# A decoder layer on one core: splitting 544 tokens 256 and 288, with the high and low halves of the first part in one 512-column product

## The chip, the cores and the metric

The kernel runs on one core of a Trainium2 chip. The metric is the device time of one launch in microseconds (us), as the median of several runs. One of the runs is taken with the hardware profiler; its page and its trace are what this document reads. The granted TensorE clock of a stretch is shown as a share of the full 2.4 GHz: 1.00 is 2.4 GHz, 0.50 is 1.2 GHz.

## What is computed

One layer of a hybrid decoder on 544 tokens (one prompt of 512 and eight samples of 4), with width 1024 and feed-forward width 2816:

```
x <- LN(alpha*x + gate0 * 0.5*SwiGLU1(mod0(x)))
x <- LN(alpha*x + gate1 * W_out[ GDN_heads(u) || ShortConv_groups(u) ])   u = mod1(x), one combined W_in
x <- LN(alpha*x + gate2 * 0.5*SwiGLU2(mod2(x)))
with mod_i(h) = h*(1+scale_i(c)) + shift_i(c),  swiglu(u) = (silu(u @ wg) * (u @ wu)) @ wd
```

Inputs and outputs are float32, the states of the recurrences among them.

## The kernel before

Activations lie with the features on the 128 partitions and the 544 tokens along the free axis; 1024 features are 8 blocks (`KC`). To get float32 accuracy from the one-pass float32r products, each weight tile is split into a high part (`whi`, cast by ScalarE, L195) and a rest (`wlo`, a VectorE subtraction, L196), and so is each activation (`uh`, `ul`; `bh`, `bl`; `hxh`, `hxl`; by `split`, L258 and L259). `mm3` (L199 to L211) then makes three products for each pair of a weight tile and a feature block: high by high, high by low, low by high, all added in one PSUM tile. The 544 tokens pass in two parts of 272 columns (`HB`), so a pair costs six products. Every product is recorded at L75, the wrapper `PE.matmul`.

```
ins = PE.matmul(o, lhsT=hi[:, i, :], rhs=xh[:, c], start=first and i == 0, stop=False)
PE.matmul(o, lhsT=hi[:, i, :], rhs=xl[:, c], start=False, stop=False)
PE.matmul(o, lhsT=lo[:, i, :], rhs=xh[:, c], start=False, stop=last and i == n - 1)
```

`ffn` (L453) runs twice. It treats the 22 blocks of the hidden width in two halves of 11. For each block, `up` makes the gate tile `pg` and the up tile `pu` for the first part of the tokens and then for the second (8 feature blocks each); ScalarE takes the Silu of `pg` (L474), VectorE multiplies it by `pu` (L476), and the product is split for the down products. For each of 8 output blocks the down products add up 11 hidden blocks, and `residual` (L414) adds the PSUM tile, times the gate, to the residual `z` on VectorE (L419; the 32 sample tokens apart, L422 and L425). So a feed-forward block has 22 x 2 x 8 up pairs and 16 x 11 down pairs, 528 in all, and the two have 1056.

The last three output blocks of a feed-forward block (the last four of the mixer) pass through `finish_stage` (L428), where the layer norm's sums are formed while the last products run: `ln_shift` (L307) for both parts, then per block `ln_sums` (L333), then `ln_stats` (L338), whose two product groups `aux<-s` and `aux<-v` stand between the products of the second part on TensorE and wait for VectorE's sums (L335, L304).

The `mixer` (L520) makes the projections with `proj` (L544), convolutions on VectorE, the gated delta rule, and for the eight samples a chain of rounds that load a state (`s0u`), update it and write it out; each round has its products `vm,kd` on TensorE. One of the short-convolution tiles (`wide`, L553, asked for at L1047 for j == 3) is made with 512 + 32 columns for its first four feature blocks and 364 + 148 + 32 for the other four, instead of 272 + 272. `out_proj` (L1120) then reads the saved residual back from DRAM (`ax_d`) and rescales it on GpSimd (L410).

PSUM has four `acc` tiles, two that swing between uses, and two `aux` tiles. A scheduler (Tile) fixes each engine's order at build time; engines run their own lists in order and wait on one another by semaphores.

Of the kernel before, what the change touches and what calls it, by code (L numbers as in the profile page):

```python
# [23 lines left out]
HB = T // 2  # L24
HP = TP - HB
# [38 lines left out]
def trunk_step(ctx: ExitStack, tc: tile.TileContext, xin, cin, par_d, cst_d, msk_d, wada, wg1, wu1,  # L64
# [134 lines left out]
    def mm3(pt, w, x, ks, hf, first=True, last=True, pin=None):  # L199
        hi, lo = w  # L200
        c = slice(hf * HB, (hf + 1) * HB)
        n = len(ks)
        for i, k in enumerate(ks):
            o = pt[:, 0:HB]
            xh, xl = x(k)
            ins = PE.matmul(o, lhsT=hi[:, i, :], rhs=xh[:, c], start=first and i == 0, stop=False)
            if pin and k in pin:
                after(ins, pin[k], "the next group's modulation first")
            PE.matmul(o, lhsT=hi[:, i, :], rhs=xl[:, c], start=False, stop=False)
            PE.matmul(o, lhsT=lo[:, i, :], rhs=xh[:, c], start=False,  # L210
                      stop=last and i == n - 1)  # L211
# [13 lines left out]
    uh = acts.tile([P, KC, T], F32R, name="uh")  # L225
    ul = acts.tile([P, KC, T], F32R, name="ul")
    bh = acts.tile([P, KC, T], F32R, name="bh")
    bl = acts.tile([P, KC, T], F32R, name="bl")
    ax_d = dram.tile([P, KC, T], F32, name="ax_d")
    rs_d = dram.tile([P, 2, HB], F32, name="rs_d")  # L230
# [14 lines left out]
    def uin(k):  # L245
        return uh[:, k, :], ul[:, k, :]

    def heads(k):
        return bh[:, k, :], bl[:, k, :]
# [48 lines left out]
    def acc_squares(v2, x, n, first):  # L298
        if first:
            A.activation(v2[:, 0:n], x, AF.Square)  # L300
            return
        sqk = st["pool"].tile([P, 2, HB], F32, tag="sqk", name="sqk")
        A.activation(sqk[:, 0:n], x, AF.Square)
        V.tensor_tensor(v2[:, 0:n], v2[:, 0:n], sqk[:, 0:n], ALU.add)  # L304


    def ln_shift(hf, nd):  # L307
        z, lnp = st["z"], st["pool"]
        c = slice(hf * HB, (hf + 1) * HB)
        s1 = lnp.tile([P, HB], F32, tag="s1", name="s1")  # L310
# [4 lines left out]
        sr = lnp.tile([P, HB], F32R, tag="ms", name="s1r", bufs=1)  # L315
        A.copy(sr, s1)
        pm = aux()
        PE.matmul(pm[:, 0:HB], lhsT=st["oned"], rhs=sr, start=True, stop=True)
        m1 = lnp.tile([P, HB], F32, tag="rs", name="m1")
        A.mul(m1, pm[:, 0:HB], float(KC) / nd)  # L320
        v2 = lnp.tile([P, 2, HB], F32, tag="v2", name="v2")
        for k in range(0, nd, 2):
            n = min(2, nd - k)
            zz = z[:, k:k + n, c]
            V.tensor_tensor(zz, zz, m1.unsqueeze(1).to_broadcast([P, n, HB]), ALU.subtract)  # L325
            acc_squares(v2, zz, n, k == 0)
# [6 lines left out]
    def ln_sums(k, hf, sv):  # L333
        c = slice(hf * HB, (hf + 1) * HB)
# [3 lines left out]
    def ln_stats(i, hf, sv):  # L338
        z, lnp = st["z"], st["pool"]
        c = slice(hf * HB, (hf + 1) * HB)  # L340
        s1, v2 = sv
        pm, pv = aux(), aux()
        PE.matmul(pm[:, 0:HB], lhsT=cst["oned"], rhs=s1, start=True, stop=True)
        PE.matmul(pv[:, 0:HB], lhsT=cst["oned"], rhs=v2[:, 0], start=True, stop=True)
        rs = lnp.tile([P, HB], F32, tag="rs", name="rs")
        a, nt = v2[:, 0], v2[:, 1]
        A.activation(nt, pm[:, 0:HB], AF.Square)
        ms = lnp.tile([P, HB], F32, tag="ms", name="ms", bufs=1)
        A.copy(ms, pm[:, 0:HB])
        V.scalar_tensor_tensor(a, pv[:, 0:HB], LN_EPS, nt, ALU.add, ALU.subtract)  # L350
# [3 lines left out]
        for k in range(0, 4, 2):  # L354
            zz = z[:, k:k + 2, c]
            V.tensor_tensor(zz, zz, pm[:, 0:HB].unsqueeze(1).to_broadcast([P, 2, HB]), ALU.subtract)
# [7 lines left out]
    def ln_apply(i, hf, q, pr_):  # L364
        z, lnp = st["z"], st["pool"]
        c = slice(hf * HB, (hf + 1) * HB)
        if i == 2:
            for k0 in range(0, KC, 2):
                ks = (k0, k0 + 1)
                zz = z[:, k0:k0 + 2, c]  # L370
                rr = pr_.unsqueeze(1).to_broadcast([P, 2, HB])
# [10 lines left out]
        np_ = HB if hf == 0 else HP  # L382
        pc = slice(hf * HB, hf * HB + np_)
        for k in range(KC):
            u = lnp.tile([P, HB], F32, tag="lnu", name="lnu", bufs=3)
# [10 lines left out]
            if hf and k == 0:  # L396
# [3 lines left out]
                                pr_[:, HP:HB].unsqueeze(1).to_broadcast([P, KC, TS]), ALU.mult)  # L400
# [5 lines left out]
    def ln_residual(i, hf, q, rb):  # L406
        z = st["z"]
        c = slice(hf * HB, (hf + 1) * HB)
# [5 lines left out]
    def residual(d, hf, pd, i):  # L414
        z = st["z"]
        gt = mod[:, i * 3 + 2, d, :]
        np_ = HB if hf == 0 else HP
        pc = slice(hf * HB, hf * HB + np_)
        V.scalar_tensor_tensor(z[:, d, pc], pd[:, 0:np_], gt[:, 0:1], z[:, d, pc], ALU.mult, ALU.add)  # L419
        if hf:  # L420
            t4 = tmp.tile([P, 8, 4], F32, tag="zs", name="zs")
            V.tensor_tensor(t4, pd[:, HP:HB].rearrange("p (b t) -> p b t", t=4), bc4(gt[:, 1:9]),  # L422
# [5 lines left out]
    def finish_stage(i, nd, half_of, q, fill):  # L428
# [14 lines left out]
        if i == 0:  # L443

            nc.sync.dma_start(out=rs_d[:, 0, :], in_=ra)
            nc.sync.dma_start(out=rs_d[:, 1, :], in_=rb)
            for hf in range(2):
                c = slice(hf * HB, (hf + 1) * HB)
# [4 lines left out]
    def ffn(i, wg, wu, wd, extra, pre, fill):  # L453
        pool = st["pool"]
        xh = pool.tile([P, NFH - KC, T], F32R, tag="hxh", name="hxh", bufs=1)
        xl = pool.tile([P, NFH - KC, T], F32R, tag="hxl", name="hxl", bufs=1)

        def hid(k):
            return (bh[:, k, :], bl[:, k, :]) if k < KC else (xh[:, k - KC, :], xl[:, k - KC, :])

        def up(fs, half, extra_units):
# [5 lines left out]
            for hf in range(2):  # L467
                c = slice(hf * HB, (hf + 1) * HB)
                for f, (w1, w2) in zip(fs, us):
                    pg, pu = acc(), acc()  # L470
                    mm3(pg, w1, uin, range(KC), hf, pin=pin)
                    mm3(pu, w2, uin, range(KC), hf, pin=pin)
                    sg = pool.tile([P, HB], F32, tag="sg", name="sg")
                    A.activation(sg, pg[:, 0:HB], AF.Silu)  # L474
# [815 lines left out]
```

## Time and profile before

| | |
|---|---|
| runs | 1247.17, 1249.36 and 1244.53 us, median 1247.17 |
| profiled execution | 1243.21 us, of which the span from first to last instruction is 1241.5 us |
| granted TensorE clock, mean | 0.983 |
| TensorE (PE) busy | 1181.2 us, 95% of the span |
| VectorE (DVE) busy | 637.9 us, 51% |
| ScalarE (ACT) busy | 451.8 us, 36% |
| chain that ended last | PE 77%, DVE 10%, DMA 4% |

The page gives each engine's busy time, the chain of work that ended last, and groups of instructions with their count and mean duration. A product's recorded duration (about 290 ns) contains its passage through the array and overlaps its neighbours'; what a product costs in a dense stream is the distance from one start to the next, which is read from counts in a window, or from two starts. PEld is the loading of weights, which runs beside the products.

### The profile page before, as it was taken

Reading aid. Unit: us, or ns where it says so; the run is one execution under the profiler, and the core shown is the slowest. Engines: PE = TensorE matmul, PEld = TensorE weight load, DVE = VectorE, ACT = ScalarE, POOL = GpSimd, SP = SyncE. Lnnn points to the kernel's source line nnn. Section 1 sums busy time; section 2 is a strip of 40 time slices with the busy share of each in tenths; the row PEclk is TensorE's granted clock in tenths of the full one; section 3 lists DMA queues with packets and bytes.
Section 4 is the critical chain, followed back from the end, with each engine's and each line's share of the span. In section 5 each row is a group of like instructions: output and inputs, shape, how many; then the busy total and the mean of one; then the engine's idle time right before and its main releaser. Section 6 shows DMA issues by size and latency. Waiting matters only on the chain.

```text
span 1241.5 us, 22584 instructions
## 1 busy us (share of the span) xinstructions
PE 1181.2 (95%) x9238; PEld 1123.7 (91%) x9238; DVE 637.9 (51%) x1449; ACT 451.8 (36%) x975; POOL 119.4 (10%) x168
## 2 busy tenths in 40 slices
PE   5999999999999989999999999869999999999994
PEld 2888889998999988989999888769999999999994
DVE  4533333333333488758787674993333343333467
ACT  3432222223332245744663324563322222322243
POOL 0000000000000034111120003560000000000024
PEclk9999999999999989999999999889999999999997
DMA  9876554355322224331332454123322333322222
GB/s 348 281 279 226 201 183 150 97 170 204 87 80 71 82 89 156 95 105 47 88 88 72 120 158 156 37 70 101 97 70 71 95 105 94 95 77 77 71 58 72
DMA packets 69383, 149.66 MB, mean 121 GB/s; under 512 B 12576, under 2 KB 33312, under 8 KB 69280
## 3 DMA queue, kind: packets, MB, share of 16 engines
q1 hardware_dynamic: 69280, 148.23, 37.8%
q8 instruction: 72, 1.18, 0.4%
q14 instruction: 31, 0.25, 0.1%
HBM read 139.07 MB, written 9.14 MB: 119 GB/s over the span
## 4 chain that ended last, share of the span: by engine, by line
PE 77%; DVE 10%; DMA 4%; issue 3%; POOL 2%; ACT 2%; SPq 1%; DVEq 0%; POOLq 0%; ACTq 0%
PE acc L75 49%; PE accs L75 19%; PE aux L75 6%; PE auxs L75 2%; DMA xt<-xt_d 1%; DVE wlo L196 1%; PE aux L80 1%; POOL z L410 1%; DMA out_ss<-s0u 1%; DVE ct L679 1%; DVE pb L757 1%; DVE z L325 1%; DVE lnu L386 1%; DMA z<-in_x 1%; POOL z L353 1%
## 5 line engine op out<-in xcount | busy, mean ns | idle before, releaser
L75 PE MATMUL acc<-uh,wlo 128*128 128x272 f32 (+1 forms) x1404 | 406.5, 291 | 7.8 <-DVE wlo L196 7.8
L75 PE MATMUL acc<-uh,whi 128*128 128x272 f32 (+1 forms) x1404 | 411.5, 295 | 1.2 <-ACT uh L258 1.2
L75 PE MATMUL acc<-ul,whi 128*128 128x272 f32 (+1 forms) x1404 | 405.8, 291 | 1.0 <-POOL ul L391 0.4
L195 ACT CAST whi<-raw 128x512 fp32r<-128x512 f32 (+2 forms) x366 | 198.3, 574 | 338.4 <-PE acc L75 203.7
L196 DVE TENSOR_TENSOR wlo<-raw,whi 128x512 fp32r<-128x512 f32 (+2 forms) x366 | 229.4, 645 | 170.6 <-ACT whi L195 162.5
L75 PEld LDWEIGHTS acc<-uh,whi 128*128 128x128 f32 x1404 | 264.8, 189 | 16.1 <-DVE wlo L196 7.5
L75 PEld LDWEIGHTS acc<-uh,wlo 128*128 128x128 f32 x1404 | 264.4, 189 | 10.6 <-DVE wlo L196 9.5
L75 PEld LDWEIGHTS acc<-ul,whi 128*128 128x128 f32 x1404 | 265.1, 189 | 2.6 <-POOL ul L391 0.9
L75 PE MATMUL accs<-uh,wlo 128*128 128x272 f32 x440 | 127.4, 290 | 3.7 <-DVE wlo L196 3.7
L75 PE MATMUL accs<-ul,whi 128*128 128x272 f32 x440 | 127.3, 289 | 0.6 <-DVE ul L259 0.6
L75 PE MATMUL accs<-uh,whi 128*128 128x272 f32 x440 | 127.5, 290 | 0.0
L75 PE MATMUL acc<-bl,whi 128*128 128x272 f32 x416 | 120.4, 290 | 1.2 <-DVE bl L259 1.2
L75 PE MATMUL acc<-bh,whi 128*128 128x272 f32 x416 | 120.9, 291 | 0.0
L75 PE MATMUL acc<-bh,wlo 128*128 128x272 f32 x416 | 120.2, 289 | 0.0
L476 DVE TENSOR_TENSOR h<-acc,sg 128x272 f32<-128x272 f32 x62 | 27.4, 442 | 148.5 <-PE acc L75 147.5
L328 POOL TENSOR_TENSOR z<-z,m 128x272 f32<-128x272 f32 x20 | 22.6, 1162 | 774.1 <-ACT m L320 773.3
L75 PEld LDWEIGHTS accs<-uh,wlo 128*128 128x128 f32 x440 | 83.3, 189 | 4.2 <-DVE wlo L196 4.2
L75 PEld LDWEIGHTS accs<-uh,whi 128*128 128x128 f32 x440 | 83.4, 190 | 1.9 <-ACT oned_r L277 0.8
L75 PEld LDWEIGHTS accs<-ul,whi 128*128 128x128 f32 x440 | 83.3, 189 | 0.8 <-DVE ul L259 0.8
L75 PEld LDWEIGHTS acc<-bl,whi 128*128 128x128 f32 x416 | 78.9, 190 | 1.6 <-DVE bl L259 1.4
L75 PEld LDWEIGHTS acc<-bh,whi 128*128 128x128 f32 x416 | 78.8, 190 | 1.3 <-DVE hxl L259 0.8
L75 PEld LDWEIGHTS acc<-bh,wlo 128*128 128x128 f32 x416 | 78.7, 189 | 0.0
(395 smaller groups left out, 1752.6 us busy)
## 6 DMA issues: line engine op xcount, KB each, us to landing
raw_ada<-in_wada SPq DMA_DIRECT2D x72, 512.0 KB, 6.5
raw<-in_wg SPq DMA_DIRECT2D x44, 512.0 KB, 4.1
raw<-in_wu SPq DMA_DIRECT2D x44, 512.0 KB, 3.7
raw<-in_win SPq DMA_DIRECT2D x29, 512.0 KB, 3.8
raw<-in_wd SPq DMA_DIRECT2D x32, 384.0 KB, 3.2
raw<-in_wd SPq DMA_DIRECT2D x32, 320.0 KB, 2.9
raw<-in_wout SPq DMA_DIRECT2D x8, 512.0 KB, 3.8
z<-in_x SPq DMA_DIRECT2D x8, 272.0 KB, 7.6
```

The costliest lines, as they stand in the source:

```text
L75: return nc.tensor.matmul(out, lhsT=lhsT, rhs=rhs, **kw)
L80: return nc.tensor.transpose(out, x, ident)
L195: A.copy(hi[:, a:b], raw[:, a:b])
L196: V.tensor_tensor(lo[:, a:b], raw[:, a:b], hi[:, a:b].bitcast(F32), ALU.subtract)
L325: V.tensor_tensor(zz, zz, m1.unsqueeze(1).to_broadcast([P, n, HB]), ALU.subtract)
L328: G.tensor_tensor(z[:, k, c], z[:, k, c], m1, ALU.subtract)
L353: G.tensor_tensor(z[:, k, c], z[:, k, c], ms, ALU.subtract)
L386: V.scalar_tensor_tensor(u[:, 0:np_], z[:, k, pc], q["G"][:, k, 0:1], pr_[:, 0:np_], ALU.mult, ALU.mult)
L410: G.tensor_tensor(z[:, k, c], z[:, k, c], rb, ALU.mult)
L476: V.tensor_tensor(h, pu[:, 0:HB], sg, ALU.mult)
L679: V.scalar_tensor_tensor(ct, cb[:, s:s + 568], w[:, s:s + 1], ct, ALU.mult, ALU.add)
L757: V.tensor_tensor(t[:, b], a[:, b].unsqueeze(2).to_broadcast([32, s, s, s]), x[:, b].rearrange("p k c -> p c k").unsqueeze(1).to_broadcast ...
```

## The change

The split of the tokens becomes 256 and 288 (`HP`, `HW`, `CUT`). The high and low halves of an activation become one tile with two planes (`ux`, `bx`, `hx`). In the two feed-forward blocks (`side=True`) the first part of a pair takes two products instead of three: the high weights times both planes as one moving operand of two runs of 256 columns, which fills a PSUM tile of 512; and the low weights times the high plane, added to the upper half of that tile. The two halves of the tile are added later: in `up` by two ScalarE copies and two VectorE additions, in `residual` by a second pass of its VectorE instruction. The second part, the mixer and the output projection keep three products for each pair and part, of 288 and 256 columns. The short-convolution tile in pieces goes.

```
 def mm3(pt, w, x, ks, hf, first=True, last=True, pin=None, side=False):
...
+            if side and hf == 0:
+                ops = [(hi, xx[:, :, c], pt.rearrange("p (s t) -> p s t", s=2)),
+                       (lo, xx[:, 0, c], pt[:, HP:2 * HP])]
+            else:
+                ops = [(hi, xx[:, 0, c], o), (hi, xx[:, 1, c], o), (lo, xx[:, 0, c], o)]
+            for m, (wt, rhs, out) in enumerate(ops):
+                ins = PE.matmul(out, lhsT=wt[:, i, :], rhs=rhs, start=begin and m == 0,
+                                stop=end and m == len(ops) - 1)
...
 def residual(d, hf, pd, i, side=False):
...
-        V.scalar_tensor_tensor(z[:, d, pc], pd[:, 0:np_], gt[:, 0:1], z[:, d, pc], ALU.mult, ALU.add)
+        for n in range(2 if side and hf == 0 else 1):
+            V.scalar_tensor_tensor(z[:, d, pc], pd[:, n * HP:n * HP + np_], gt[:, 0:1], z[:, d, pc],
+                                   ALU.mult, ALU.add)
...
 def up(fs, half, extra_units):
...
-                    A.activation(sg, pg[:, 0:HB], AF.Silu)
-                    h = pool.tile([P, HB], F32, tag="h32", name="h32", bufs=3)
-                    V.tensor_tensor(h, pu[:, 0:HB], sg, ALU.mult)
+                    h = pool.tile([P, HW[hf]], F32, tag="h32", name="h32")
+                    if hf == 0:
+                        A.copy(sg, pg[:, HP:2 * HP])
+                        A.copy(h, pu[:, HP:2 * HP])
+                        V.tensor_tensor(sg, pg[:, 0:HP], sg, ALU.add)
+                        A.activation(sg, sg, AF.Silu)
+                        V.tensor_tensor(h, pu[:, 0:HP], h, ALU.add)
+                        V.tensor_tensor(h, h, sg, ALU.mult)
+                    else:
+                        A.activation(sg, pg[:, 0:HW[hf]], AF.Silu)
+                        V.tensor_tensor(h, pu[:, 0:HW[hf]], sg, ALU.mult)
...
-            pb = yield from proj(16 + j, wide=j == 3)
+            pb = yield from proj(16 + j)
```

On TensorE, in the up products of a feed-forward block, the stream of one tile passes from the first part of the tokens to the second like this. First before (each pair a triple of 272 columns; the names are the PSUM tile, then activation and weight), then in the change:

```order
L75 MATMUL acc<-uh,whi 128x272
L75 MATMUL acc<-ul,whi 128x272
L75 MATMUL acc<-uh,wlo 128x272
L75 MATMUL acc<-uh,whi 128x272
L75 MATMUL acc<-ul,whi 128x272
```

```order
L77 MATMUL acc<-ux,whi 128x512
L77 MATMUL acc<-ux,wlo 128x256
L77 MATMUL acc<-ux,whi 128x512
L77 MATMUL acc<-ux,wlo 128x256
L77 MATMUL acc<-ux,whi 128x288 x2
L77 MATMUL acc<-ux,wlo 128x288
L77 MATMUL acc<-ux,whi 128x288 x2
```

A pair has now two products in the first part and three in the second, where there were three and three.

On ScalarE, in the second feed-forward block, the order around one hidden block in the change (L485 and L486 are the copies from the gate and the up tile, L488 the Silu of the sum, L266 the split of the product, L197 the casting of weights, L492 the Silu of the second part):

```order
L485 COPY sg<-acc 128x256
L488 ACTIVATE sg<-sg 128x256
L486 COPY h_9441<-acc 128x256
L266 CAST bx<-h_9441 128x256
L197 CAST whi<-raw 128x512
L492 ACTIVATE sg<-accs 128x288
```

The Silu of the first part now waits for a VectorE addition, and the weight cast stands behind it.

On TensorE at the end of the second feed-forward block, before and in the change, the sums' products `aux<-s` and `aux<-v` stand among the down products of the second part (`bh`, `bl`, `bx`, `hx` are the hidden blocks):

```order
L75 MATMUL accs<-bl,whi 128x272
L75 MATMUL accs<-bh,wlo 128x272
L75 MATMUL aux<-s_13306,cst_oned 128x272
L75 MATMUL aux<-v_13317,cst_oned 128x272
L75 MATMUL accs<-bh,whi 128x272
```

```order
L77 MATMUL accs<-bx,whi 128x288 x2
L77 MATMUL accs<-bx,wlo 128x288
L77 MATMUL accs<-hx,whi 128x288
L77 MATMUL aux<-s_12464,cst_oned 128x256
L77 MATMUL aux<-v_12475,cst_oned 128x256
L77 MATMUL accs<-hx,whi 128x288
```

Before, they stand behind 12 products of the second part; now they stand behind 25. On VectorE the second passes of `residual` (three in this stage, L428) stand ahead of the last sums that they wait for.

## Rows read from the trace of the kernel before

**Rows 1.** The page: busy time; then the chain that ended last, by engine.

```profile
PE 1181.2 (95%) x9238; PEld 1123.7 (91%) x9238; DVE 637.9 (51%) x1449; ACT 451.8 (36%) x975; POOL 119.4 (10%) x168
...
PE 77%; DVE 10%; DMA 4%; issue 3%; POOL 2%; ACT 2%; SPq 1%; DVEq 0%; POOLq 0%; ACTq 0%
```

**Rows 2.** Windows: stretch, length, busy us (instructions) per engine, clock, DMA share, GB/s.

```profile
200.00:300.00 100.00, 100.00 (x800) 95.24 (x799) 37.26 (x89) 26.17 (x55) 0.00 (x0) 1.00 0.43 136
1100.00:1200.00 100.00, 100.00 (x801) 100.00 (x800) 40.42 (x93) 29.34 (x66) 0.00 (x0) 1.00 0.26 75
```

**Rows 3.** The chain that ended last, pieces in order of time: start, us, what.

```profile
838.54 6.02 PE acc L75 x48
```

**Rows 4.** Timeline of TensorE around the tile in pieces: start, us, engine, what.

```profile
734.88 0.29 PE L75 MATMUL acc<-uh,wlo 128*128 128x272 f32 x1
735.01 0.41 PE L75 MATMUL acc<-uh,whi 128*128 128x512 f32 x2
...
736.66 0.51 PE L75 MATMUL acc<-uh,whi 128*128 128x512 f32 x2
737.02 0.49 PE L75 MATMUL acc<-ul,whi 128*128 128x512 f32 x2
...
738.05 0.50 PE L75 MATMUL acc<-ul,whi 128*128 128x512 f32 x2
...
742.06 0.54 PE L75 MATMUL acc<-ul,whi 128*128 128x364 f32 x3
742.45 0.54 PE L75 MATMUL acc<-uh,wlo 128*128 128x364 f32 x3
```

**Rows 5.** Timeline of the weight loads of the same tile.

```profile
735.24 0.30 PEld L75 LDWEIGHTS acc<-ul,whi 128*128 128x128 f32 x2
...
737.34 0.19 PEld L75 LDWEIGHTS acc<-uh,wlo 128*128 128x128 f32 x1
...
737.45 0.19 PEld L75 LDWEIGHTS acc<-uh,wlo 128*128 128x128 f32 x1
737.68 0.30 PEld L75 LDWEIGHTS acc<-uh,whi 128*128 128x128 f32 x2
```

**Rows 6.** Groups by shape, VectorE and ScalarE, 900 to 1000 us: busy, mean ns | idle before.

```profile
L476 DVE TENSOR_TENSOR h<-acc,sg 128x272 f32<-128x272 f32 x6 | 2.7, 442 | 15.6 <-PE acc L75 15.6
...
L419 DVE SCALAR_TENSOR_TENSOR z<-acc,mod,z 128x272 f32<-128x272 f32 x3 | 1.5, 501 | 7.8 <-PE acc L75 7.8
...
L474 ACT ACTIVATE sg<-acc 128x272 f32<-128x272 f32 x6 | 2.4, 396 | 3.5 <-PE acc L75 3.5
```

**Rows 7.** The chain that ended last, at the mixer's end.

```profile
743.81 3.67 DMA s0u<-in_ssm
...
749.46 3.92 DMA out_ss<-s0u
754.39 3.15 DMA z<-ax_d
757.62 11.60 POOL z L410 x15
```

**Rows 8.** Timeline of TensorE at the sums of both blocks; the bracket is its wait.

```profile
457.42 1.27 PE L75 MATMUL aux<-s,cst_oned 128*128 128x272 f32 x2 [3.32 <-DVE s L335]
...
1213.45 0.98 PE L75 MATMUL aux<-s,cst_oned 128*128 128x272 f32 x2 [3.36 <-DVE s L335]
```

**Rows 9.** The chain that ended last, after the last down product.

```profile
1227.26 0.47 DVE z L419
...
1229.94 0.44 DVE v L350
...
1233.79 2.00 DVE z L372 x3
```

**Rows 10.** Windows: the opening of the second feed-forward block, and cold stretches (columns as in rows 2).

```profile
800.00:850.00 50.00, 38.58 (x259) 35.89 (x259) 42.97 (x75) 30.63 (x67) 24.59 (x26) 0.90 0.25 74
...
828.10:831.50 3.40, 3.08 (x12) 2.76 (x12) 3.40 (x7) 1.69 (x6) 2.29 (x3) 0.50 0.53 154
1213.80:1217.20 3.40, 3.40 (x14) 3.05 (x13) 1.74 (x4) 1.10 (x3) 1.98 (x3) 0.50 0.00 0
```

**Rows 11.** What TensorE waited for, 795 to 840 us: total, times, longest.

```profile
PE acc L75 <- DVE wlo L196: 7.0, 5, 3.7
PE accs L75 <- DVE wlo L196: 2.0, 1, 2.0
```

More of the change, by code (lines that the diff above doesn't have):

```diff
@@ L23 @@
 T = TP + TS
-HB = T // 2
-HP = TP - HB
+HP = 256
+HW = (HP, T - HP)
+CUT = (slice(0, HP), slice(HP, T))
 NF = 22
@@ L197, in unit, with mm3 @@
         return hi, lo
-    def mm3(pt, w, x, ks, hf, first=True, last=True, pin=None):
+    def mm3(pt, w, x, ks, hf, first=True, last=True, pin=None, side=False):
         hi, lo = w
-        c = slice(hf * HB, (hf + 1) * HB)
+        c = CUT[hf]
         n = len(ks)
+        o = pt[:, 0:HW[hf]]
         for i, k in enumerate(ks):
[L204 to L211, printed above, removed]
+            xx = x(k)
+            begin, end = first and i == 0, last and i == n - 1
+            if side and hf == 0:
[6 more added lines that the diff above has]
+                                stop=end and m == len(ops) - 1)
+                if pin and k in pin and m == 0:
+                    after(ins, pin[k], "the next group's modulation first")
     def rsqrt(out, x, shape, eps, scale=1.0):
@@ L381, in ln_apply @@
             return
-        np_ = HB if hf == 0 else HP
-        pc = slice(hf * HB, hf * HB + np_)
+        np_ = HP
+        pc = slice(hf * HP, hf * HP + np_)
         for k in range(KC):
-            u = lnp.tile([P, HB], F32, tag="lnu", name="lnu", bufs=3)
+            u = lnp.tile([P, HP], F32, tag="lnu", name="lnu", bufs=3)
             V.scalar_tensor_tensor(u[:, 0:np_], z[:, k, pc], q["G"][:, k, 0:1], pr_[:, 0:np_],
@@ L407, in ln_residual @@
         z = st["z"]
[L408 removed]
+        c = CUT[hf]
         for k in range(KC):
@@ L506, in half_of @@
                         pd = acc()
-                        mm3(pd, wa, hid, range(0, 6), hf, last=False)
-                        mm3(pd, wb, hid, range(6, NFH), hf, first=False)
-                        residual(d, hf, pd, i)
+                        mm3(pd, wa, hid, range(0, 6), hf, last=False, side=True)
+                        mm3(pd, wb, hid, range(6, NFH), hf, first=False, side=True)
+                        residual(d, hf, pd, i, side=True)
                         if landed:
@@ L542, in mixer, with proj @@
         ahead = []
-        def proj(j, pre=None, wide=False):
+        def proj(j, pre=None):
             while plan and len(ahead) < (1 if pre else 2):
@@ L552, in proj @@
                 w, out = pre
-            if wide:
-                out = [acc(), acc()]
-                for k in range(KC):
-                    cuts = (0, 512, T) if k < 4 else (0, 364, 512, T)
-                    (xh_, xl_), hi, lo = uin(k), w[0][:, k, :], w[1][:, k, :]
-                    for n, (wt, x) in enumerate(((hi, xh_), (hi, xl_), (lo, xh_))):
-                        for a, b in zip(cuts, cuts[1:]):
-                            o = out[0][:, a:b] if b <= 512 else out[1][:, 0:TS]
-                            PE.matmul(o, lhsT=wt, rhs=x[:, a:b], start=k + n == 0,
-                                      stop=k == KC - 1 and n == 2 and b > 364)
-                    yield
-                return out
             for hf in range(len(out), 2):
@@ L1120, in out_proj @@
     def out_proj():
-        rs = st["pool"].tile([P, 2, HB], F32, tag="rsr", name="rsr", bufs=1)
-        nc.sync.dma_start(out=rs, in_=rs_d)
+        rs = st["pool"].tile([P, 2, HW[1]], F32, tag="rsr", name="rsr", bufs=1)
+        for hf in range(2):
+            nc.sync.dma_start(out=rs[:, hf, 0:HW[hf]], in_=rs_d[:, hf, 0:HW[hf]])
         for k in range(KC):
```

129 lines of the change are left out of this document (60 added, 69 removed).

## The prediction

> **What bounds the kernel now.** I read the page's busy times first, then the chain that ended last, then windows, then single starts. TensorE is busy for 95% of the span and makes 77% of the chain [rows 1]; VectorE has 51%, ScalarE 36%. The windows say where this holds: in a dense stretch of a feed-forward block TensorE is never idle, at the full granted clock of 2.4 GHz, and 100 us hold 800 or 801 products, while VectorE is busy for 37 to 40 us of 100 and ScalarE for 26 to 29 [rows 2]. That is 125 ns a product; the chain has 48 of them in 6.02 us, 125.4 ns [rows 3]. So in these stretches a removed product counts in full, and work added to VectorE or ScalarE is free as long as it stays in that gap. At three places it is the other way round: the opening of the second feed-forward block, where VectorE is busy for 43 of 50 us and TensorE for 39 [rows 10] and waits for weight splits [rows 11], and the two ends of the feed-forward blocks, where TensorE waits 3.36 us for the sums in the second and 3.32 in the first [rows 8].
>
> **The change, part by part.**
>
> *The pairs.* A pair now has five products for six, of as many columns in all: before 6 x 272 = 1632, now 512 + 256 + 3 x 288 = 1632. So all depends on how the cost of a product grows with its columns, and the trace has a row: the tile in pieces. A 512-column product starts at 735.01 straight behind the 272s [rows 4], and the weights for the product after its 32-column companion begin to load at 735.24, as that companion begins [rows 5]: 0.23 us for 512 columns. Once more, loads at 737.45 and 737.68: 0.23. From the cycles: four from 736.66 to 738.05 give 0.348 each, of which the companion takes the 0.11 between two loads (737.34, 737.45), which leaves 0.238. Rounding and spread leave 227 to 240 ns. I take 233, between the direct reading and the cycles. Against 125.4 for 272 that is (233 - 125.4) / 240 = 0.448 ns a column, so 118.2 for 256 and 132.6 for 288. A pair: 233 + 118.2 + 3 x 132.6 = 749.0 ns, where six products cost 752.4. Over 1056 pairs (528 in each feed-forward block) the gain is 3.4 ns x 1056 = **-3.6 us**. The ends: at 227 the slope is 0.423, the pair 742.2, the sum -10.8 us; at 240 it is 0.478, 756.8, and +4.6 us. That the moving operand comes in two runs has no row; the nearest, two products of 256 at 118.2 each, makes 236, inside these ends.
>
> Here a rule speaks for far more. The Trainium skill ("TensorE: Matmul & The Clock Gate", section "Back-to-back issue gap") states that in a sustained stream of weight loads and products a 128-column product takes about 81 ns and a 512-column one about 131. An estimate from its line, 131 + 98 + 3 x 102 against 6 x 100, would be some 65 ns less for a pair, about -69 us. No row agrees: the trace has 125.4 for 272 and 0.23 us for 512. The measurement decides; the mechanism that this would need is rival B.
>
> *Evacuation.* Each first part of a hidden block adds two ScalarE copies (nearest row 396 ns, the Silu of a PSUM tile) and two VectorE additions (442 ns) [rows 6]; each first down tile a second pass of L419 (501 ns). A hidden block takes 16 pairs, 12.0 us, and gains 0.8 us of ScalarE and 0.9 of VectorE, 7% each on 26 to 29 and 37 to 40. I cost this at nothing: TensorE's own stream covers it, with six PSUM tiles in turn (some 3 us of products each). What it could hold up is the queue behind the Silu on ScalarE, which now waits for a VectorE addition while a weight cast stands behind it; but weights are held for two hidden blocks, 24 us, and the delay is about 1 us. Without that cover it would be 1 us for a hidden block.
>
> *The tile in pieces.* Its 12 cycles of 0.348 and 12 of 0.39 (742.06 to 742.45 [rows 4]) make 8.9 us; 48 ordinary products make 6.0. TensorE gains 2.8 us here, but the chain then runs over the state rounds' DMAs to 753, the reload of the residual and 11.60 us of GpSimd [rows 7], and TensorE waits for that. What can shorten the chain is a round's own products coming a little earlier. Between 0 and -2.8 I take **-0.7 us**, near the zero, since the chain's rows here are DMAs.
>
> *The ends of the feed-forward blocks.* Three second passes of L419, 1.5 us on a VectorE that has no gap there. Before, TensorE reaches the sums behind 99 + 12 products (13.9 us from the stage's first); now behind 33 first-part pairs (351 ns each, 11.6 us) and 25 products of 132.6 (3.3), 14.9 us: 1.0 us of the 1.5 passes beside its own work. Instructions on 256 columns instead of 272 give back some tenths. So the wait of 3.36 grows by 0 to 1.5; I take 0.3 at each of two ends, **+0.6 us**.
>
> *The opening of the second feed-forward block.* Three hidden blocks are taken together there, six more additions (2.6 us). In the order they stand behind the weight splits that TensorE waits for, as L476 did; I take 0, with 2.6 as the upper end.
>
> *The tail.* After the last down product VectorE works on the second part alone [rows 9]; some 8 us of its chain go by columns, and 288 for 272 is 6% more: **+0.4 us**. Elsewhere a longer second part is a shorter first.
>
> The sum is -3.6 - 0.7 + 0.6 + 0.4 = **-3.3 us** on the profiled execution's 1243.2, so 1239.9. That execution lies 4.0 us under the median of the three runs, 1247.2; against the median, by which I forecast, it is **1244 us**. Half a per cent, 6.2 us, is about what a measurement of this kernel can tell from no change: faster means under 1240.9, slower above 1253.4.
>
> **The rivals.**
>
> *A. A fixed price for each product.* 272 columns at 2.4 GHz are 113.3 ns; the other 12 would be a price for each product, whatever its width. Then 512 costs 225.3, a pair saves 12.1 ns, 1056 of them 12.8 us, and with the other terms (+0.3) the time is 1234.7. For it: the 12 ns are there in every window at full clock. Against it: the 0.23 and 0.238 of the wide row, both above 0.225. Chance 0.20.
>
> *B. The 125 ns are the weight load, not the columns.* If a product of up to 300 columns waits for its weights, 256 and 288 stay at 125.4 and only the 512 is dearer: 233 + 4 x 125.4 = 734.6, 17.8 ns for a pair, 18.8 us in all, 1228.7. For it: PEld is busy for 95 to 100 us in 100 [rows 2]. Against it: two loads follow one another in 0.11 us when nothing else holds them [rows 5]. Chance 0.07.
>
> *C. The price goes by columns alone.* 512 / 272 x 125.4 = 236 ns, a pair costs 752 as before, and 0.3 us is left of everything: 1247.5. For it: the cycles' 0.238. Chance 0.13.
>
> *D. Slower: VectorE is the bound at the three places, and the clock pays too.* If nothing of the added passes is hidden there, the two ends cost 1.5 each and the opening 2.6. After a wait TensorE goes on at 1.2 GHz for a stretch: 828.1 to 831.5 and 1213.8 to 1217.2 are such, 3.4 us at 0.50 [rows 10]. Should each of the three longer waits bring one more such stretch, whose work would take 1.7 us at full clock, that is 5.1 us more. With the pairs, the tile in pieces and the tail (-3.9) the sum is 5.6 + 5.1 - 3.9 = +6.8, 1254.0. It decides from the point at which the wait for the sums grows past 4.5 us. For it: VectorE is without a gap from 1200 on. Against it: TensorE now reaches the sums 1.0 us later by itself. Chance 0.15.
>
> **How the numbers follow.** The forecast has 0.45; its own range, with the ends of the pairs, is 1237 to 1252. Faster: A, B, and the low end of the forecast's range, 0.20 + 0.07 + 0.06 = 0.33. Slower: nearly all of D, 0.14. No change: the rest, 0.53. The range for 8 in 10 leaves out B and the upper part of D: 1231 to 1254.
>
> **What would show it.** The pairs: in a dense window the first part's eight pairs of a tile take 2.81 us (16 products) and the second part's 24 products 3.18; under rival A 2.75 and 3.17, under B 2.87 and 3.01, under C 2.83 and 3.19. The ends: TensorE's wait for the sums (L343 there) at 3.4 to 4; over 4.5 with a longer cold stretch behind it is D. The tile in pieces: the chain at the mixer's end still over the residual's reload, 0 to 1 us earlier. The forecast is wrong if TensorE has new waits in dense windows (below 100 of 100 us), or if a 512-column product costs under 227 or over 240 ns.

## The result and the profile after

The changed kernel takes 1236.72 us in the median of 7 runs (1233.04 to 1241.24), the kernel before 1245.63 (7 runs, 1244.03 to 1249.36). The ratio is 0.9927 with a 95% interval of 0.9907 to 0.9948: 6.5 to 11.6 us less. Three repeats beside the experiments below, each against its own runs of the kernel before, gave 0.9956 (0.9938 to 0.9974), 0.9950 (0.9936 to 0.9965) and 0.9946 (0.9934 to 0.9957). So the gain is nearer to 0.5% than to 0.7%. The forecast was 1244 in a range of 1231 to 1254.

The profiled execution took 1238.01 us, its span 1236.4. That is 5.1 us less than the span of before. A profiled execution is a single one: that of before (1243.21 us) lay 2.4 us under the 1245.63 of its kernel, this one 1.3 us over its own median. The page, busy time and chain, answers to [rows 1]:

```profile
PE 1175.7 (95%) x8170; PEld 1068.7 (86%) x8170; DVE 686.5 (56%) x1570; ACT 485.5 (39%) x1063; POOL 116.9 (9%) x168
...
PE 79%; DVE 9%; DMA 4%; issue 3%; POOL 2%; ACT 2%; SPq 0%; DVEq 0%; POOLq 0%; ACTq 0%
```

TensorE has 1068 instructions fewer and only 5.5 us less to do: the columns are as many as before. VectorE has 49 us more, ScalarE 34, and the span is shorter all the same, so most of it was covered. The windows show where (columns as in [rows 2]):

```profile
300.00:400.00 100.00, 100.00 (x673) 92.36 (x673) 41.30 (x86) 35.63 (x82) 0.00 (x0) 1.00 0.30 96
...
1000.00:1100.00 100.00, 100.00 (x671) 94.05 (x670) 44.15 (x90) 35.82 (x79) 0.00 (x0) 1.00 0.30 95
```

TensorE still has no gap at full clock. The timeline of one down tile in the second feed-forward block (block 2) gives the prices; it is read from start to start:

```profile
952.72 0.39 PE L77 MATMUL acc<-bx,whi 128*128 128x512 f32 x1
952.95 0.28 PE L77 MATMUL acc<-bx,wlo 128*128 128x256 f32 x1
953.07 0.40 PE L77 MATMUL acc<-bx,whi 128*128 128x512 f32 x1
...
956.57 0.43 PE L77 MATMUL acc<-bx,whi 128*128 128x288 f32 x2
...
959.75 0.43 PE L77 MATMUL acc<-hx,whi 128*128 128x288 f32 x2
```

0.23 us for 512 columns, 0.12 for 256. The 11 first parts from 952.72 to 956.57 take 350 ns each, the 8 second parts from 956.57 to 959.75 397.5: 747.5 ns a pair. Averaged over all starts from 850 to 1195 us: 232.3 for 512, 117.4 for 256, 132.5 for 288, a pair 747.1; before, 125.3 for 272 and 752.0 for a pair. That is 4.9 ns a pair, **5.2 us if all 1056 pairs had it**, which is an estimate.

The wait for the sums, answering to [rows 8], became shorter at both ends, not longer:

```profile
457.60 0.70 PE L77 MATMUL aux<-s,cst_oned 128*128 128x256 f32 x2 [2.66 <-DVE s L343]
...
1209.03 0.70 PE L77 MATMUL aux<-s,cst_oned 128*128 128x256 f32 x2 [2.69 <-DVE s L343]
```

The sums themselves come later than before. The stage's first sum product, `aux<-s1r`, starts in block 2 at these times, first before, then in the change:

```profile
1199.74 0.28 PE L75 MATMUL aux<-s1r,oned_r 128*128 128x272 f32 x1
```

```profile
1194.79 0.28 PE L77 MATMUL aux<-s1r,oned_r 128*128 128x256 f32 x1
```

From there to the `aux<-s` that waits it is 13.71 us before and 14.24 in the change (13.69 and 14.22 in block 1). TensorE comes to that place 1.2 us later than before, the sums 0.5 us later, so the wait is 0.7 us shorter.

To see where time goes I divided every profile at the same places on TensorE: the starts of the first sum product `aux<-s1r` at each block's end, of the second `aux<-s` of block 1, and of the first down product of block 2. Distances in us (the sum of a line is its span; "repeats" are the other three profiles of the changed kernel):

```
                         to s1r    block 1's  mixer to   opening of  dense    last
                         block 1   end        its s1r    block 2     block 2  stage
before                   443.73    31.94      301.11     178.90      244.06   41.76
changed                  443.38    29.99      300.94     178.42      242.07   41.58
repeats, lowest          441.57    30.01      301.37     178.30      242.07   41.58
repeats, highest         444.30    30.11      302.09     179.06      242.07   42.88
x2 no pieces             443.36    31.05      303.78     179.96      244.06   41.79
x1 split only            444.59    31.04      301.02     182.70      243.00   42.47
x3 unmerged              443.86    33.47      302.08     178.69      243.00   42.63
x4 no sums               443.47    30.90      299.55     181.65      242.07   42.04
x5 three where bound     443.32    32.00      299.31     182.18      242.12   42.32
x7 one run               442.49    28.75      300.60     179.70      242.11   40.45
```

The dense column repeats to 0.01 us and block 1's end to 0.1; the others move by 0.8 to 2.7 us between executions of one kernel, in which stretches at 1.2 GHz lie differently. The changed kernel's first stage has such a stretch at 25.4 us, as its repeats have, which before lacks. x7's two ends are 1.2 and 1.1 us shorter than the change's: its granted clock is 1.00 from 442.5 to 471.2 and from 1193.6 to 1223 us, where the change has 3.4 us at 0.50 in each.

The dense column holds 330 first parts and 319 second parts, since it ends behind a first part. Of its 2.0 us, 0.3 come from the 11 first parts more, and 1.7 are left for 319 pairs, 5.3 ns each (the average above, 4.9, has more up products in it). The gain isn't the same everywhere: the 88 pairs of its first down stage gain 7.0 ns each (66.18 to 65.56 us), the 176 of its up stage, which read `ux` and not `bx` and `hx`, 3.9 (132.37 to 131.69). The same stretch of block 1, from its first down product to its `aux<-s1r`, takes 253.32 us in all four profiles of the changed kernel and 254.66 before, 1.3 us less, 3.3 ns a pair. With that price for block 1's half of the pairs the estimate of 5.2 us becomes some 4.3; 3.3 us are seen in these two stretches. Block 1's first up stage shows no gain: 167.2 to 167.7 us in the four profiles, 167.0 before.

The tail, from the start of the last down product, is this (before, then the change with the rows that answer to [rows 9]):

```profile
1226.86 0.29 PE L75 MATMUL acc<-hxh,xlo 128*128 128x272 f32 x1
```

```profile
1221.21 0.30 PE L77 MATMUL acc<-hx,xlo 128*128 128x288 f32 x1
```

```profile
1221.63 0.48 DVE z L428
...
1224.38 0.46 DVE v L358
...
1228.44 2.10 DVE z L380 x3
```

To the end of the span it is 14.6 us before and 15.2 in the change.

### The profile page after: what moved, and what is told of

The parts are those of the page before. It is cut to its first block, busy times and chain, and to the rows that moved or that the text cites. A ratio compares the mean times of both kernels' runs of the same rounds, so it can differ in the third digit from the quotient of the medians.

```text
span 1236.4 us, 20642 instructions
## 1 busy us (share of the span) xinstructions
PE 1175.7 (95%) x8170; PEld 1068.7 (86%) x8170; DVE 686.5 (56%) x1570; ACT 485.5 (39%) x1063; POOL 116.9 (9%) x168
## 4 chain that ended last, share of the span: by engine, by line
PE 79%; DVE 9%; DMA 4%; issue 3%; POOL 2%; ACT 2%; SPq 0%; DVEq 0%; POOLq 0%; ACTq 0%
PE acc L77 50%; PE accs L77 19%; PE aux L77 5%; PE auxs L77 3%; DMA raw_ada<-in_wada 2%; DMA xt<-xt_d 1%; PE aux L82 1%; POOL z L418 1%; DMA xt_d<-xbt 1%; DVE lnu L394 1%; DVE wlo L198 1%; DVE pb L761 1%; DVE z L333 1%; POOL z L361 1%; DVE v L312 1%
## 5 line engine op out<-in xcount | busy, mean ns | idle before, releaser
L77 PE MATMUL acc<-ux,whi 128*128 128x288 f32 (+2 forms) x2312 | 549.7, 320 | 2.7 <-ACT ux L266 1.6
L77 PEld LDWEIGHTS acc<-ux,whi 128*128 128x128 f32 x2312 | 384.3, 190 | 41.0 <-DVE wlo L198 7.5
L77 PE MATMUL acc<-ux,wlo 128*128 128x256 f32 (+1 forms) x1400 | 407.4, 291 | 7.5 <-DVE wlo L198 7.5
L197 ACT CAST whi<-raw 128x512 fp32r<-128x512 f32 (+2 forms) x366 | 198.1, 574 | 322.5 <-PE acc L77 186.1
L77 PEld LDWEIGHTS acc<-ux,wlo 128*128 128x128 f32 x1400 | 267.0, 191 | 9.5 <-DVE wlo L198 8.6
L77 PE MATMUL accs<-ux,whi 128*128 128x288 f32 (+2 forms) x680 | 169.0, 325 | 0.5 <-DVE ux L267 0.5
L77 PE MATMUL acc<-bx,whi 128*128 128x288 f32 (+2 forms) x672 | 159.7, 319 | 1.3 <-ACT bx L266 1.3
L77 PE MATMUL accs<-ux,wlo 128*128 128x288 f32 (+1 forms) x440 | 126.9, 289 | 1.7 <-DVE wlo L198 1.7
L77 PEld LDWEIGHTS accs<-ux,whi 128*128 128x128 f32 x680 | 114.7, 189 | 11.5 <-issue 1.7
L77 PEld LDWEIGHTS acc<-bx,whi 128*128 128x128 f32 x672 | 112.5, 190 | 9.4 <-ACT bx L266 1.5
L77 PE MATMUL acc<-bx,wlo 128*128 128x256 f32 (+1 forms) x416 | 119.9, 288 | 0.0
L428 DVE SCALAR_TENSOR_TENSOR z<-acc,mod,z 128x256 f32<-128x256 f32 x76 | 36.3, 480 | 50.6 <-PE acc L77 47.7
```

Of the source, the lines that this page charges most:

```text
L77: return nc.tensor.matmul(out, lhsT=lhsT, rhs=rhs, **kw)
L197: A.copy(hi[:, a:b], raw[:, a:b])
L428: V.scalar_tensor_tensor(z[:, d, pc], pd[:, n * HP:n * HP + np_], gt[:, 0:1], z[:, d, pc], ALU.mult, ALU.add)
```

## The experiments

**x1: the split alone.** mm3, `up` and `residual` never take the merged branch.

```
-            if side and hf == 0:
+            if False:
```

> The change with the merging taken out: tokens split 256 and 288, three products a pair and part everywhere, no sums afterwards, no tile in pieces. Theory 1 (what a dense product costs, as read from the profile of the changed kernel: 117.4 ns for 256 columns, 132.5 for 288, 232.3 for 512, against 125.3 for 272): a pair costs 749.6 ns instead of 752.0, so 2.5 us of the gain come from the uneven split alone; with the removed tile in pieces (0 to 2.8 us) the time is 3 to 5 us under the kernel before, and 2.5 to 3 us above the changed kernel. Rival (a fixed price of some 8 ns a product, so that the whole gain of about 9 us is the 1056 products saved): the time is that of the kernel before, within 1 us. Rival (the tile in pieces and the ends carry the gain): the time is that of the changed kernel.

Measured: 1246.15 us against 1245.6 (ratio 1.0007, 0.9995 to 1.0019). The time is that of the first rival, but not for its reason: the dense windows do what theory 1 says, 117.7 and 132.2 ns, 749.7 a pair, and 243.00 in the dense column. Theory 1's total is missed all the same, and the second rival's too: nothing is gained, since the opening of block 2 is 3.8 us longer than before. That was no part of any theory; x4 and x5 take it up.

**x3: two products of 256 for the one of 512**, sums and all else as in the change.

```
-                ops = [(hi, xx[:, :, c], pt.rearrange("p (s t) -> p s t", s=2)),
+                ops = [(hi, xx[:, 0, c], pt[:, 0:HP]), (hi, xx[:, 1, c], pt[:, HP:2 * HP]),
```

> The changed kernel with the one product of 512 columns made as two of 256 into the same two halves of the tile; the sums afterwards and everything else as in the change. Theory 1: two products of 256 cost 234.8 ns, one of 512 cost 232.3, so the time is 2.6 us above the changed kernel. Rival (fixed price of about 8 ns a product): 8 to 9 us above it, the time of the kernel before. Rival (merging is worth nothing): the time of the changed kernel within 0.5 us.

Measured: 1245.04 us, ratio 0.9994 (0.9982 to 1.0006), where the changed kernel, run beside it, had 0.9956 (0.9938 to 0.9974). The difference is 0.0038, with the two half-widths added in squares 0.0022 either way, so 2 to 7.5 us: theory 1's 2.6 is inside, 8 to 9 and nothing are not. The dense column gives the size without that spread: 243.00 to 242.07, 0.93 us in 330 first parts, 2.8 ns each, **3.0 us if all 1056 had it**. The same stretch of block 1 goes from 254.01 to 253.32, 0.69 us, 2.1 ns each.

**x2: the kernel before without the tile in pieces.** `wide=j == 3` becomes `wide=False`, with the ordinary reading of the result.

> The kernel before with the convolution tile in pieces made as ordinary 272-column products, nothing else changed. Theory 1: 0.7 us less than the kernel before (0 to 2.8), because TensorE then waits at the mixer's end for DMAs and GpSimd. Rival (the removed pieces carry what the pairs do not explain): 2.8 us or more less.

Measured: 1244.16 us, ratio 0.9985 (0.9972 to 0.9998): 0.2 to 3.5 us less, 1.9 in the middle. The interval holds both 0.7 and 2.8, so it doesn't part them. It lies wholly below 1, so something of the 2.8 arrives.

**The changed kernel again**, three times, as the control of each set of runs.

> The changed kernel once more, for its time on the same chip and in the same runs as the others, and for a second profile of it. Theory 1: 5 to 6 us under the kernel before, and products of 232, 117 and 132 ns in dense windows again. Rival (the profiled execution understates the gain): 9 us under it, with the additional 3 to 4 us to be found in stretches outside the dense windows.

> The changed kernel once more as the control for these runs. Theory 1: 5 to 6 us under the kernel before.

> The changed kernel as the control of these runs: 5 to 7 us under the kernel before.

Measured: 1239.84, 1239.05 and 1238.06 us, 5.5, 6.2 and 6.7 us under the kernel before by the ratios. Products of 232.3, 117.4 and 132.5 ns again, 242.07 in the dense column each time. The rival's 9 us stay outside all three intervals.

**x4: no sums.** The copies, the additions and the second pass in `residual` are taken out.

```
-                        A.copy(sg, pg[:, HP:2 * HP])
-                        A.copy(h, pu[:, HP:2 * HP])
-                        V.tensor_tensor(sg, pg[:, 0:HP], sg, ALU.add)
-                        A.activation(sg, sg, AF.Silu)
-                        V.tensor_tensor(h, pu[:, 0:HP], h, ALU.add)
-                        V.tensor_tensor(h, h, sg, ALU.mult)
+                        A.activation(sg, pg[:, 0:HP], AF.Silu)
+                        V.tensor_tensor(h, pu[:, 0:HP], sg, ALU.mult)
```

> The changed kernel without the sums of the two halves: it leaves out the two ScalarE copies and two VectorE additions of each first part and the second pass in the residual, so the products with the low halves are missing from the first part of the feed-forward blocks; TensorE's work is all there. Theory 1 (TensorE's stream hides the sums in the dense windows): dense windows as in the changed kernel, and a total within 1.5 us of it, the difference at the two ends of the blocks and the opening of the second block. Rival (the evacuation costs what it adds wherever it stands): 1 us for each of 44 hidden blocks, tens of us less.

Measured: 1241.48 us (ratio 0.9964, 0.9951 to 0.9976), the control 1239.05 (0.9950, 0.9936 to 0.9965). That is 2.4 us above it, more than theory 1's 1.5, though the two intervals overlap; the rival's tens of us less are refuted. Without 83 us of work on two engines the kernel isn't faster, and the dense column is the same 242.07. In the dense windows the sums cost nothing. The opening of block 2 is longer here too, by 3.2 us against the changed kernel. At the end of block 2:

```profile
1197.64 0.28 PE L77 MATMUL aux<-s1r,oned_r 128*128 128x256 f32 x1
...
1211.09 0.70 PE L77 MATMUL aux<-s,cst_oned 128*128 128x256 f32 x2 [3.23 <-DVE s L343]
```

13.45 us from one to the other, where the change and x3, which have the second passes, take 14.24 and 14.23. So the passes put the sums off by 0.8 us. TensorE waits longer here than in the change all the same, since it has 15 products of the second part ahead of the sums and not 25.

**x5: three products where VectorE is late.** `side` is true only for groups of one block.

```
+            side = len(fs) == 1
...
-                    mm3(pg, w1, uin, range(KC), hf, pin=pin, side=True)
...
+                    mm3(pg, w1, uin, range(KC), hf, pin=pin, side=side)
...
-                        mm3(pd, wa, hid, range(0, 6), hf, last=False, side=True)
...
+                        mm3(pd, wa, hid, range(0, 6), hf, last=False, side=len(ds) == 1)
```

> The changed kernel with three products and no sums where VectorE is late: in the three hidden blocks that open the second feed-forward block and in the last three output blocks of both; 114 of the 1056 first-part pairs. Theory 1: the pairs cost 114 x 2.5 ns = 0.3 us more; nine VectorE passes fewer at the ends and the opening give back 0 to 3 us, so 0 to 2.5 us under the changed kernel. Rival (the order in which the weight splits and the modulated activations stand on VectorE sets the opening, not the number of sums): within 1 us of the changed kernel either way, or above it, as the opening was longer in the run that had no sums at all.

Measured: 1243.13 us, ratio 0.9975 (0.9964 to 0.9986) against the control's 0.9950 (0.9936 to 0.9965): some 3 us more, a miss of theory 1 and what the rival said. The waits of TensorE from 800 to 845 us, first the changed kernel, then x5 (engine and line, what it waited for, total, times, longest):

```profile
PE acc L77 <- DVE wlo L198: 7.5, 3, 5.6
PE accs L77 <- ACT xhi L197: 2.8, 1, 2.8
PE accs L77 <- DVE xlo L198: 0.4, 1, 0.4
```

```profile
PE acc L77 <- DVE wlo L198: 9.1, 2, 4.8
PE accs L77 <- ACT xhi L197: 4.1, 1, 4.1
```

With fewer instructions on VectorE and ScalarE the weight splits come later. The order that the scheduler writes differs. On VectorE, in the changed kernel a pair of `wlo` stands ahead of two modulated activations and three scalings (`ux`, `lnu`); in x5 those stand first (the changed kernel, then x5):

```profile
824.15 1.88 DVE L198 TENSOR_TENSOR wlo<-raw,whi 128x512 fp32r<-128x512 f32 x2
825.96 1.35 DVE L402 SCALAR_TENSOR_TENSOR ux<-lnu,lnH,ux 128x256 fp32r<-128x256 f32 x2
827.23 1.81 DVE L394 SCALAR_TENSOR_TENSOR lnu<-z,lnG,rs 128x256 f32<-128x256 f32 x3
```

```profile
826.87 1.00 DVE L394 SCALAR_TENSOR_TENSOR lnu<-z,lnG,rs 128x256 f32<-128x256 f32 x1 [0.62 <-POOL ux L399]
827.80 1.41 DVE L402 SCALAR_TENSOR_TENSOR ux<-lnu,lnH,ux 128x256 fp32r<-128x256 f32 x2
829.13 0.87 DVE L394 SCALAR_TENSOR_TENSOR lnu<-z,lnG,rs 128x256 f32<-128x256 f32 x2
829.92 2.48 DVE L198 TENSOR_TENSOR wlo<-raw,whi 128x512 fp32r<-128x512 f32 x2
```

At the ends the order differs too: x5's sums stand behind 13 products of the second part, not 25, and TensorE waits longer:

```profile
1212.37 0.70 PE L77 MATMUL aux<-s,cst_oned 128*128 128x256 f32 x2 [3.22 <-DVE s L343]
```

So the longer opening goes with another order in x5. The clock isn't what makes it longer: the opening has 20.5 us at 1.2 GHz in the change, in x4 and in x5 alike, and 27.3 in x2, whose opening takes 180.0 us. That the order is the cause, and that the scheduler chose these places because it counts the sums as work, is likely but not shown: no run kept the work and moved the order.

**x6: products behind the end**, when nothing else works. Streams of one shape, each product with its own weight load.

```
+    for n_, m_ in ((512, 64), (0, 48), (512, 48), (288, 48), (272, 48), (256, 48), (160, 48), (64, 48)):
...
+        for j in range(m_):
...
+            tc.keep_in_program_order(PE.matmul(out, lhsT=pw[:, j % 4, :], rhs=x_, start=j == 0,
+                                               stop=j == m_ - 1))
```

> The changed kernel with streams of products added behind everything else, when no other engine and no DMA works: 64 and 48 of 512 columns in one run, 48 of 512 in two runs of 256, and 48 each of 288, 272, 256, 160 and 64, each with weights of its own to load. The total is some 90 to 130 us longer; what is read is the distance from start to start at full clock. Theory 1 (about 2.7 ns a product and 0.449 ns a column): 232.5, 232.5, 132, 125, 117.6, 107 to 110 (the weight load) and 107 to 110. Rival (a fixed price of 12 ns and 2.4 columns a ns): 225, 225, 132, 125.3, 118.7. Rival (the products are slowed by the other engines' and the DMAs' traffic): 216, 216, 122, 116, 109. Rival (two runs cost more than one): the second 512 above the first.

The timeline (a row holds one or two streams of its PSUM tile; n_ = 0 is 512 columns in two runs, the row at 1255.42):

```profile
1238.13 17.46 PE L77 MATMUL acc<-bx 128*128 128x512 f32 x64 [9.47 <-ACT bx L1186]
1255.42 11.36 PE L77 MATMUL accs<-bx 128*128 128x512 f32 x48
1266.62 17.36 PE L77 MATMUL acc<-bx 128*128 128x512 f32 x96
1283.82 6.17 PE L77 MATMUL accs<-bx 128*128 128x272 f32 x48
1289.83 11.24 PE L77 MATMUL acc<-bx 128*128 128x256 f32 x96
```

48 products of two runs take 11.20 us, 233.3 each; by their single starts, one run of 512 takes 226.7, 288 takes 131.7, 272 125.2 (6.01 us for 48 here), 256 120.0 and 160 111.7. So the traffic of the other engines isn't what slows the products: 272 costs the same here as in the kernel. Theory 1 misses the 226.7 and the 120.0. The four prices from 256 to 512 are 12 to 13 ns above the columns at 2.4 GHz, as the fixed price of rival A in the prediction has it, and the price of two runs is 6.7 ns above that of one, as the last rival says. (The run took 1310.19 us, some 70 more than the change, where 90 to 130 were expected.) From this came theory 2.

**x7: the 512 columns in one run.** The tiles `ux`, `bx`, `hx` hold the two halves of the first part side by side, then those of the second.

```
-                ops = [(hi, xx[:, :, c], pt.rearrange("p (s t) -> p s t", s=2)),
-                       (lo, xx[:, 0, c], pt[:, HP:2 * HP])]
+                ops = [(hi, xx.rearrange("p s t -> p (s t)"), pt),
+                       (lo, xx[:, 0], pt[:, HP:2 * HP])]
```

> The changed kernel with the activations stored so that the 512 columns lie in one run: for each feature block first the high and the low half of the first part (256 and 256), then those of the second (288 and 288); the products, the sums and the removed tile are as in the change, the splitting of the first input goes in two pieces for each feature block. Theory 2 (from the streams behind the end: one run of 512 takes 226.7 ns, two runs of 256 take 233.4, a product has a fixed price of some 9 to 12 ns): the 512-column product falls from 232.3 to about 226, over 1056 pairs 6 to 7 us less than the changed kernel. Rival (in the kernel, with other engines and DMAs at work, a product takes what its columns take, about 0.45 ns each, in one run or two): the time of the changed kernel within 1 us and 232 ns again.

Measured: 1236.62 us, ratio 0.9937 (0.9922 to 0.9951), the control 1238.06 (0.9946, 0.9934 to 0.9957); the dense column 242.11 against 242.07, the 512-column product 233.0 ns. Theory 2's 6 to 7 us and its 226 ns aren't there. The ratio is lower than the control's, but not apart from it. The dense column hides two effects that nearly cancel: its up stage is 0.65 us shorter than the change's (131.04 against 131.69), its two down stages together 0.69 us longer (65.98 and 45.09 against 65.56 and 44.82). The same stretch of block 1 is 0.46 us shorter (252.86 against 253.32). So the one run gains in some stages and loses in others, and why is open.

**x8: other runs behind the end.** As x6, with 512 columns as two, four and eight runs, and 256 at two places.

> The changed kernel with other streams behind the end, each product with weights of its own: 64 of 512 columns in one run, then 48 each of 512 as two runs of 256, four of 128 and eight of 64, of 256 columns from the start of a row, from column 256, and as two runs of 128, and of 288 from column 256. Theory 2 (each further run costs 6.7 ns): 226.7, 233.4, 246.8, 273.5, then 120, 120, 126.7 and 131.7. Rival (the two runs were slow for where they lie, not for their number): 233 for the four and the eight runs as well. Rival (the start column decides, as the 120.0 against 117.5 of the kernel suggest): the two single runs of 256 differ by some 2.5 ns.

```profile
1251.00 11.36 PE L77 MATMUL accs<-bx 128*128 128x512 f32 x48
1262.20 22.56 PE L77 MATMUL acc<-bx 128*128 128x512 f32 x96
1284.59 5.92 PE L77 MATMUL accs<-bx 128*128 128x256 f32 x48
1290.35 11.58 PE L77 MATMUL acc<-bx 128*128 128x256 f32 x96
```

Two runs 233.3 (11.20 / 48), and the 96 of four and eight runs together 233.2 (22.39 / 96). A price for each further run is refuted. The first rival's 233 came out, but that it is for where the runs lie isn't shown by it. 256 costs 120.0 from either place, and 117.9 in two runs, less than in one.

**x9: couples and triples behind the end**, in the kernel's own alternation (the operands are put in words here).

```
+    for m_, ops in (..., (32, [512 in one run, 256]), (32, [512 in two runs, 256]), ...,
+                    (32, [512 in two runs, 256], from block to block), (16, [256, 256, 256]), (16, [272, 272, 272])):
```

> The changed kernel with streams behind the end that alternate as its own do: after 64 of 512 columns, 32 couples of 512 (one run) and 256; 32 couples of 512 (two runs) and 256; 48 of 512 in one run and 48 in two runs, each from the next of 8 feature blocks; 32 couples (two runs) that go through the feature blocks; 16 triples of 256; 16 triples of 272, each through the feature blocks. From single streams a couple would be 226.7 + 120 = 346.7 ns in one run and 353.3 in two, a triple of 256 360, one of 272 376. Theory 3 (what follows on what sets the price: in a mixed stream the couple costs what it costs in the kernel): 349 to 350 in one run and in two, 352 for the triple of 256, 376 for that of 272. Rival (the other engines' and the DMAs' traffic makes the difference in the kernel): 346.7 and 353.3 as in the single streams. Rival (moving on from block to block costs it): the two streams of 48 through the blocks above 226.7 and 233.3.

The starts of four streams (the rows at 1249.96 and 1261.25 begin the couples in one and in two runs, 1294.56 those that move from block to block, 1311.41 the triples of 272; the triples of 256 begin at 1305.76, inside the row of 1305.41):

```profile
1249.96 0.51 PE L77 MATMUL accs<-bx 128*128 128x512 f32 x2
...
1261.25 0.52 PE L77 MATMUL acc<-bx 128*128 128x512 f32 x2
...
1294.56 0.74 PE L77 MATMUL acc<-bx 128*128 128x512 f32 x3
1305.41 0.99 PE L77 MATMUL acc<-bx 128*128 128x512 f32 x6
...
1311.41 0.67 PE L77 MATMUL accs<-bx 128*128 128x272 f32 x4
```

Without the first two of each stream, a couple in one run costs 353.4 ns, in two runs 349.9 and 350.1, a triple of 256 353.6, one of 272 373.2. The single streams through the blocks stay at 227.1 and 233.4. Theory 3 holds for the couple in two runs and lies within 1.6 ns for the triple of 256. It misses the triple of 272 by 2.8 ns, and the couple in one run, which costs as much as three products of 256. Both rivals fall: the couples don't cost what their single streams add up to, and moving from block to block costs 0.4 ns at most. In this alternation, with no other engine at work, merging saves 353.6 - 350 = 3.6 ns a pair; in the kernel it was 2.8 by the dense column. What in the alternation sets the price is open.

## Why the prediction was right, and where it was not

The time fell inside the range and on the forecast's side, by more than forecast: 3.2 us were forecast, 5.5 to 6.7 measured in the repeats and 9 in the first runs. The first median, 1236.72, lies nearer to rival A's 1234.7 than to the 1244 of the forecast; it is the prices of the products, not the time, that tell the two apart. By steps:

- **TensorE's pace in the dense windows decides, and the sums there are free.** Right: 100 of 100 us busy after, and x4 takes the sums away without gaining.
- **The pairs, -3.6 us.** Right in kind, too small: 4.9 ns a pair instead of 3.4 in block 2, which makes 5.2 us, or some 4.3 with block 1's lower price. The 512-column product was forecast at 233 and measured at 232.3; the 256-column one costs 117.4 where 118.2 was interpolated, the 288 132.5 for 132.6. About 3 of the 5.2 come from merging (x3 against the change), the rest from 256 and 288 costing less together than twice 272, as x1 shows in its dense windows.
- **The ends, +0.6 us.** Wrong in sign. The waits for the sums fell from 3.32 and 3.36 to 2.66 and 2.69, 0.7 us less at each end. The step that failed: "1.0 us of the 1.5 passes beside its own work. Instructions on 256 columns instead of 272 give back some tenths. So the wait of 3.36 grows by 0 to 1.5". The second passes were put at their full 1.5 us on the way to the sums; they cost 0.8 there. From `aux<-s1r` to `aux<-s` it is 13.7 us before, 13.4 without second passes (x4, x5) and 14.2 with them (the change, x3): the 256 columns give back 0.3, the passes add 0.8, the sums are 0.5 us later. TensorE comes 1.2 us later, with 25 products of the second part ahead of the sums. In block 1's end the changed kernel needs 30.0 to 30.1 us in four profiles out of four, before 31.9 and in x2 31.1; part of that is one stretch at 1.2 GHz of 6.8 us in the profile of before and of 3.4 in x2 and the four.
- **The tile in pieces, -0.7 us.** Inside x2's 0.2 to 3.5, whose middle is 1.9; the size stays open.
- **The opening, 0.** Right for this kernel within a us: 178.4 us (178.3 to 179.1) against 178.9 and 180.0, with the gain of the column's 176 pairs in it. But the reason given doesn't hold in general: x1, x4 and x5, which have fewer sums there, need 181.7 to 182.7. That this kernel got an order in which the opening stayed short was luck as far as the prediction goes; the order is the likely cause, and not shown apart.
- **The tail, +0.4.** Right: from the start of the last down product to the end it is 14.6 us before and in x2, 15.2 in the four profiles of the change. The column of the last stage (41.6 to 42.9 against 41.8) hides it behind the shorter wait.

Rival A's fixed 12 ns would have given 12.8 us; x3 against the change excludes it in the kernel, although the single streams of x6 look just like it. B's one price for all products up to 300 columns is refuted by 117.4 and 132.5 ns for 256 and 288. C, 236 ns for 512 and no gain, is refuted by 232.3 and the dense column. D's point, a wait above 4.5 us, was not reached. The forecast gave 0.53 to no change within 0.5%; the ratio of the first runs is just clear of that (0.9948 at the upper end), the three repeats have half a per cent inside their intervals.

## What to carry to other kernels

Merging products pays only what the alternation of the real stream says: measure the pair or the triple as it stands in the loop, and in each stage of it (3.3 to 7.0 ns a pair here), not one width in a stream of its own. Work added to engines that have gaps in the dense windows was free here, tens of us of it. Where a scheduler writes the order, a kernel with less work can come out longer at a place where two engines wait on each other, as the opening did in x1, x4 and x5: compare the order there before trusting a count of instructions.

## What the runs showed of the hardware that was not expected

The price of a product depends on its neighbours and on how its columns lie. At full clock, 512 columns take 226.7 ns in one run and 233.3 in two, four or eight runs when they follow one another; followed by 256 columns, the couple in one run takes 353.4 ns and in two runs 349.9. 256 columns take 120.0 alone, 117.9 as two runs, and 117.4 in the kernel. There it also matters which tile is read: in block 2 three products of 288 take 398.3 ns on `ux`, 396.8 on `bx` and 393.3 on `hx`, in all four profiles of the change. What sets this is open. The Trainium skill ("TensorE: Matmul & The Clock Gate", section "Back-to-back issue gap") states N / 2.4 + 2.5 ns at full clock for the isolated gap of a product of N columns, which by an estimate is 215.8 for 512, and about 131 ns for 512 in a sustained stream with weight loads. The streams here, each product with a load, have 226.7 and 233.3, so neither agrees. For the low clock it states N / 1.2, and the first products of x6's stream, at 1.2 GHz, are 427 ns apart, as 512 / 1.2 says.
